# The second pair's query projection behind the first pair's search of maxima, in the tile of the exponentials' sums

## The chip, the cores and the metric

One core of one Trainium2 chip. The metric is the device time of one execution in microseconds, as the median of several runs; a profiled execution gives the trace. Engines: PE is TensorE (PEld its weight loads), DVE is VectorE, ACT is ScalarE, POOL is GpSimd, SP is SyncE, whose queue issues most DMAs.

## The reference

Two layers of a diffusion trunk over 512 latent tokens and 256 context tokens, D_MODEL 1024. Each layer mixes tokens in three branches (pooling, attention, a bidirectional gated recurrence), merges them through gates, and ends with a SwiGLU block. The change lies in the attention of the latent queries (layer 0 also runs the context's). Cut to that:

```python
N_HEADS, N_KV_HEADS, HEAD_DIM = 8, 2, 64
q = rmsnorm(q.reshape(B, L, N_HEADS, HEAD_DIM), q_norm_l)
k = rmsnorm(k.reshape(B, L, N_KV_HEADS, HEAD_DIM), k_norm_l)
if row is not None:
    q = rope_2d(q, row, col)
    k = rope_2d(k, row, col)
...
def _attend(q, k, v):
    s = jnp.einsum('bqhgd,bshd->bhgqs', q, k).astype(jnp.float32) * (HEAD_DIM ** -0.5)
    p = jax.nn.softmax(s, axis=-1).astype(v.dtype)
    return jnp.einsum('bhgqs,bshd->bqhgd', p, v)
```

Latent queries see all 768 keys; context queries (layer 0 only) see the 256 context keys. Everything is float32 at the interface.

## The kernel before, in words

Activations lie feature by feature: a tile holds 128 features by 768 tokens (256 context, then 512 latent). A product with float32 accuracy is made of three matmuls: each operand is split into a rounded part `hi` and a rest `lo` (`load_w`, `split`, `mm3`), so each block of 128x128 weights is loaded by DMA, cast on ScalarE (line 237) and subtracted on VectorE (line 239). Layer 0 works on all 768 tokens, in two segments of 256 and 512 columns, layer 1 on the 512 latent ones.

TensorE's instructions run in the order of the program. On the other engines a planner sets the order: it goes by priority (program order, weight loads lifted far ahead) and by its own simulated times. To keep TensorE busy while the attention waits for other engines, the program keeps a queue of generators of independent work, the **fillers**: the merge of the recurrence's branch and the gates of the attention's branch. `fill(us)` adds credit and emits filler stages until the credit is used up; how much credit stands at each place is written by hand in `PACE`. Filler that isn't used here is run later, so its total does not depend on these credits.

The eight heads are done in four pairs, one tile of 128 features (two heads) each. For every pair:

- `qproj(i)` makes the queries: `qgemm` (product with a 128x1024 weight tile, copied from PSUM by ScalarE, line 932), then `headnorm` (square, `fill(4.5)`, sum over the head by a matmul with `self.blk` at line 347, reciprocal root at lines 294 to 297, scaling at 349) and `rope_lat` (lines 354 to 357 on VectorE).
- `attn_max` searches the row maxima of the scores. Its first step splits the queries (ScalarE line 620, VectorE line 622, ScalarE line 624); then come matmuls at lines 633 and 641 and reductions on VectorE at lines 635 and 643, in steps; the end are four small VectorE operations (lines 647 to 650).
- `attn_rows` transposes the maxima on TensorE (line 659) and puts them into spare rows of an operand (line 662), so that the scores come out with the maximum taken off.
- `attn_pv` computes scores (lines 686, 687), exponentials (line 688, into tiles `e`, three buffers), their sums over the keys (line 690, into a tile `tot`, one buffer) and the product with the values (line 696). The next pair's search and the projection of the pair after it are worked in as hooks.

The first pair has nothing before it to hide in: `attention` splits the keys (`attn_kv`, lines 607 and 609), gives 6.0 us of credit to fillers, starts the first pair's search, projects the second pair, and then lets the search run, with filler between its steps. The second pair's queries lie in a buffer of the tag `e`; the third and fourth pair's in the tag `q`. Tiles of one tag share slots: whoever gets a slot waits for the last user of the tile before it.

Of the kernel before, what the change touches and what calls it, by code (L numbers as in the profile page):

```python
# [11 lines left out]
F32 = mybir.dt.float32  # L12
# [6 lines left out]
P = 128  # L19
# [3 lines left out]
LX = 512  # L23
T = LC + LX
# [18 lines left out]
class Trunk:  # L43
# [680 lines left out]
    def attention(self, l, k, q, qproj, full, ap, bo):  # L724

        c0 = 0 if full else LC
        F, FH, FL = PACE['att'][l], PACE['head'][l], PACE['last'][l]
        self.attn_kv(0, k, ap)
        self.fill(6.0)
        nxt = self.attn_max(0, q, full, ap)  # L730
        next(nxt)
        q = qproj(1)
        for _ in nxt:
            self.fill(PACE['seek'][l])
        self.fill(PACE['rows'][l])
        s = self.attn_rows(0, full)
        self.fill(3.0)
        late = iter(())
        for p in range(4):
            nxt = self.attn_max(p + 1, q, full, ap) if p < 3 else None  # L740
            hi, lo = bo[0][p], bo[1][p]
            oun = Lazy(lambda: self.t(ap, [P, T], F32, "ntmp", bufs=2))
            state = {}

            def hooks(i, half):
                if i > 0 and half == 0:
                    next(late, None)
                if (i, half) == (5, 0):
                    self.now(late)
                    if p < 2:  # L750
                        state["q"] = qproj(p + 2)
                if nxt is not None:
                    if (i, half) == (0, 0) or (1, 1) <= (i, half) < (4, 1):
                        next(nxt, None)
                    elif (i, half) == (4, 1):
                        for _ in nxt:
                            pass
                    elif (i, half) == (5, 1):
                        state["s"] = self.attn_rows(p + 1, full)
                if (i, half) == (3, 1) and p == 0:  # L760
                    self.attn_kv(1, k, ap)
                self.fill(0.5 * (F if nxt is not None else FL))
            sm = Lazy(lambda: self.t(ap, [P, T], F32, "sm"))
            tot = self.attn_pv(p, s, full, ap, oun, sm, hooks)
            late = self.attn_out(c0, oun.get(), tot, sm.get(), hi, lo)
            if p == 3:
                self.now(late)
            self.fill(FH)
            s, q = state.get("s"), state.get("q")
# [73 lines left out]
    def layer(self, l, full, pre):  # L843
# [72 lines left out]
        at = atp.__enter__()  # L916
# [8 lines left out]
        def early(i):  # L925
            return self.t(at, [P, 2, 512], F32, "e", bufs=3).rearrange("p a b -> p (a b)")[:, 0:T]
# [1 line left out]
        def later(i):  # L928
            return self.t(at, [P, T], F32, "ntmp", bufs=2)
        def qgemm(i, bank=None):  # L930
            q = self.t(at, [P, T], F32, "q") if i != 1 else early(0)
            self.now(self.gemm_h(self.load_w(W[22 + i], [P, KD, P]), segs, lambda s0, s1, a: nc.scalar.copy(q[:, s0:s1], a), bank))  # L932
            return q

        def qnorm(i, q):
            scratch = early if i == 0 else later
            self.headnorm(q, q, c0, self.v(l, O_QN, 1), scratch)
            self.rope_lat(q, scratch)
            return q
        q0 = qgemm(0, self.score_bank)  # L940
        self.headnorm(k, k, 0, self.v(l, O_KN, 1), early)
        self.rope_lat(k, later)
        q0 = qnorm(0, q0)

        def qproj(i):
            return qnorm(i, qgemm(i))
# [375 lines left out]
```

## Time and profile before

| | us |
|---|---|
| median of 3 runs | 2128.71 |
| lowest, highest | 2127.93, 4074.69 |
| the profiled execution's own time | 2131.06 |
| its span, first to last instruction | 2129.0 |
| TensorE busy in the span | 2064.9 |
| VectorE busy | 1133.6 |
| ScalarE busy | 681.7 |
| mean granted TensorE clock, share of full | 0.993 |

The profiled execution is 2.35 us above the median, and 2.06 us of it lie outside the span. Busy time of an engine is the time in which it executes; waits and issuing do not count. The highest of the three runs stands by itself and does not move the median.

### The profile page before, as it was taken

What the parts mean: (1) busy time and instruction counts of PE and PEld (TensorE: products, weight loads), DVE (VectorE), ACT (ScalarE), POOL (GpSimd) and SP (SyncE); (2) the same over time, 40 slices, a digit from 0 to 9 for tenths busy, and PEclk for the clock granted to TensorE, in tenths of its full rate; (3) what the DMA queues carried; (4) which work ended last, traced back from release to release, by engine and by line L of the source; (5) the groups of instructions that cost most, each with busy time, mean ns of one, the idle gap of its engine ahead of it and who ended that gap; (6) DMA issues with size and microseconds to landing.
All of it is one profiled execution on the core that took longest, in us unless ns stands there. A gap on an engine that the chain in (4) does not pass through costs nothing.

```text
span 2129.0 us, 28512 instructions
## 1 busy us (share of the span) xinstructions
PE 2064.9 (97%) x11844; PEld 1690.9 (79%) x11844; DVE 1133.6 (53%) x1699; ACT 681.7 (32%) x958; POOL 37.3 (2%) x79
## 2 busy tenths in 40 slices
PE   6998999999999999999999999999899999999999
PEld 4986778777687988888888889778666689888887
DVE  6274635766654676334433354774777665333333
ACT  5323124444332432112112234243444343222221
POOL 0010001000000000000000000001000000000000
PEclk9999999999999999999999999999999999999999
DMA  7203632222154245224423222123322352222332
GB/s 296 80 31 118 211 134 82 100 70 87 52 169 151 90 149 166 91 94 158 140 67 107 85 88 76 60 72 102 104 89 70 113 174 89 96 93 96 103 96 92
DMA packets 75744, 230.92 MB, mean 108 GB/s; under 512 B 8464, under 2 KB 8608, under 8 KB 75488
## 3 DMA queue, kind: packets, MB, share of 16 engines
q1 hardware_dynamic: 75168, 227.57, 32.0%
q8 instruction: 93, 1.52, 0.3%
q0 software_dynamic: 448, 1.54, 0.2%
q14 instruction: 35, 0.29, 0.0%
HBM read 209.16 MB, written 19.92 MB: 108 GB/s over the span
## 4 chain that ended last, share of the span: by engine, by line
PE 88%; DVE 7%; DMA 2%; ACT 2%; issue 1%; SPq 0%; POOL 0%; DVEq 0%; ACTq 0%
PE g L266 64%; PE g L1084 5%; PE att L1084 2%; PE att L377 2%; PE pv L696 2%; PE g L1040 2%; DMA ada<-in_w_ada_dram 1%; PE att L434 1%; PE att L169 1%; DVE AT L473 1%; PE att L686 1%; PE att L687 1%; DVE lo L239 1%; PE att L641 1%; ACT hi L237 1%
## 5 line engine op out<-in xcount | busy, mean ns | idle before, releaser
L266 PE MATMUL g<-h,hi 128*128 128x256 f32 (+1 forms) x3792 | 1002.7, 360 | 8.1 <-ACT e L932 2.8
L266 PEld LDWEIGHTS g<-h,hi 128*128 128x128 f32 x3792 | 673.4, 189 | 150.4 <-issue 33.0
L266 PE MATMUL g<-h,lo 128*128 128x256 f32 (+1 forms) x1896 | 591.2, 355 | 0.0
L237 ACT CAST hi<-raw 128x1024 fp32r<-128x1024 f32 (+1 forms) x237 | 245.4, 1037 | 848.0 <-PE g L266 526.7
L239 DVE TENSOR_TENSOR lo<-raw,hi 128x1024 fp32r<-128x1024 f32 (+1 forms) x237 | 285.6, 1206 | 320.4 <-ACT hi L237 313.3
L266 PEld LDWEIGHTS g<-h,lo 128*128 128x128 f32 x1896 | 358.9, 189 | 50.3 <-issue 2.2
L1098 DVE SCALAR_TENSOR_TENSOR x<-g,mod,x 128x256 f32<-128x256 f32 (+1 forms) x64 | 42.4, 682 | 164.1 <-PE g L266 144.3
L266 PE MATMUL g<-uh,hi 128*128 128x512 f32 (+1 forms) x416 | 129.5, 358 | 0.0
L266 PE MATMUL g<-ul,hi 128*128 128x512 f32 (+1 forms) x416 | 129.5, 358 | 0.0
L266 PE MATMUL g<-uh,lo 128*128 128x512 f32 (+1 forms) x416 | 129.4, 358 | 0.0
L1000 DVE TENSOR_TENSOR sa<-sa,g 128x512 f32<-128x512 f32 (+1 forms) x43 | 35.1, 818 | 169.2 <-PE g L266 168.0
L210 DVE SCALAR_TENSOR_TENSOR junk<-adar,cb 128x1024 f32<-128x1024 f32 x64 | 78.3, 1223 | 36.0 <-DMA adar<-in_w_adaT_dram 35.1
L266 PEld LDWEIGHTS g<-uh,hi 128*128 128x128 f32 x416 | 78.2, 188 | 11.6
L266 PEld LDWEIGHTS g<-uh,lo 128*128 128x128 f32 x416 | 78.2, 188 | 11.6
L266 PEld LDWEIGHTS g<-ul,hi 128*128 128x128 f32 x416 | 78.2, 188 | 11.5
L688 ACT ACTIVATE e<-att 128x512 f32<-128x512 f32 x104 | 56.3, 595 | 90.8 <-PE att L687 90.5
L473 DVE COPY_PREDICATED AT<-masks,att 128x512 f32<-128x512 uint8 (+1 forms) x84 | 48.9, 631 | 14.3 <-PE att L434 14.2
L696 PE MATMUL pv<-e,Vv 128*64 128x512 f32 (+1 forms) x224 | 56.1, 585 | 0.0
L266 PE MATMUL g<-boa,hi 128*128 128x512 f32 (+1 forms) x192 | 52.1, 357 | 1.4 <-DVE tanh L836 1.4
L434 PE MATMUL att<-qq,K 64*128 64x128 f32 x560 | 43.3, 295 | 9.3 <-DVE qq L462 7.0
L434 PEld LDWEIGHTS att<-qq,K 64*128 64x128 f32 x560 | 36.9, 189 | 18.0 <-issue 13.7
L377 PE MATMUL att<-vhi,h 128*128 128x384 f32 x192 | 49.5, 336 | 0.0
(351 smaller groups left out, 2587.4 us busy)
## 6 DMA issues: line engine op xcount, KB each, us to landing
raw<-in_w_fi_dram SPq DMA_DIRECT2D x88, 512.0 KB, 3.5
raw<-in_w_in_dram SPq DMA_DIRECT2D x84, 512.0 KB, 3.5
adar<-in_w_adaT_dram SPq DMA_DIRECT2D x48, 512.0 KB, 4.2
ada<-in_w_ada_dram SPq DMA_DIRECT2D x64, 256.0 KB, 4.0
raw<-in_w_fo_dram SPq DMA_DIRECT2D x34, 448.0 KB, 3.3
raw<-in_w_out_dram SPq DMA_DIRECT2D x18, 512.0 KB, 4.2
ada<-in_w_ada_dram SPq DMA_DIRECT2D x16, 512.0 KB, 10.2
raw<-in_w_fo_dram SPq DMA_DIRECT2D x16, 512.0 KB, 3.5
```

Of the source, the lines that this page charges most:

```text
L210: i = nc.vector.scalar_tensor_tensor(out=junk, in0=raw, scalar=1.0, in1=cb[:, v, :], op0=ALU.mult, op1=ALU.mult, accum_out=rows[:, f, v:v ...
L237: nc.scalar.copy(hi, raw)
L239: nc.vector.tensor_sub(lo, raw, hi.bitcast(F32))
L266: nc.tensor.matmul(ps.part(s0, s1), w, x[:, s0:s1], start=(first and i == 0), stop=(last and i == 2))
L377: nc.tensor.matmul(ps[:, :384], self.h[x][kk][:, c], w[:, kk, :], start=(kk == 0 and i == 0), stop=(kk == KD - 1 and i == 2))
L434: nc.tensor.matmul(pt[hd][:, i, :], K(ph, g0 + i), Q(ph, g0 + i), start=True, stop=True)
L473: scores(plain(K), lambda ph, c: pick(qq, c * P, P, h, ph), grow, lambda o, i, n: nc.vector.copy_predicated(o, mk.to_broadcast([P, n, P]), i))
L688: nc.scalar.activation(e[:, o, :], pst, AF.Exp, scale=0.125)
L696: nc.tensor.matmul(out[64 * o:64 * o + 64, :n], w(sk), es[i][:, o, u * n:(u + 1) * n], start=(start and u == 0), stop=(stop and u == len(j ...
L1040: nc.tensor.matmul(o, w[:, kk, :], self.h[x][kk][:, tg[0]:tg[1]], start=(kk == 0 and i == 0), stop=(kk == KD - 1 and i == 2))
L1084: self.nc.tensor.matmul(ps, w[:, i, :], xs[y][:, g0:g1], start=(i == 0 and k == 0), stop=(i == nk - 1 and k == 2))
L1098: self.nc.vector.scalar_tensor_tensor(out=x[:, s0:s1], in0=ps, scalar=g[:, d, v:v + 1], in1=x[:, s0:s1], op0=ALU.mult, op1=ALU.add)
```

## The change

`qproj(1)` is moved from before the steps of the first pair's search to behind them, and its result is put into the first 768 elements of a tile of the tag `tot`, in place of one of the tag `e`. The search's first step, the split of the first pair's queries, stays where it is. In `attention`, `qproj(1)` was followed by the search's steps; now it stands between them and the credit `PACE['rows']`.

```diff
         nxt = self.attn_max(0, q, full, ap)
         next(nxt)
-        q = qproj(1)
         for _ in nxt:
             self.fill(PACE['seek'][l])
+        q = qproj(1)
         self.fill(PACE['rows'][l])
         s = self.attn_rows(0, full)
...
         def qgemm(i, bank=None):
-            q = self.t(at, [P, T], F32, "q") if i != 1 else early(0)
+            q = self.t(at, [P, T], F32, "q") if i != 1 else self.t(at, [P, 2, LX], F32, "tot").rearrange("p a b -> p (a b)")[:, 0:T]
```

The credits are unchanged: `PACE['seek']` is 2.0 us a step in layer 0 and 1.2 in layer 1 (seven steps and six), `PACE['rows']` is 3.0 and 3.5.

## Rows read from the trace of the kernel before

**Rows 1.** The profile's page: busy time of the engines, and the chain that ended last.

```profile
PE 2064.9 (97%) x11844; PEld 1690.9 (79%) x11844; DVE 1133.6 (53%) x1699; ACT 681.7 (32%) x958; POOL 37.3 (2%) x79
...
PE 88%; DVE 7%; DMA 2%; ACT 2%; issue 1%; SPq 0%; POOL 0%; DVEq 0%; ACTq 0%
```

**Rows 2.** Timeline of TensorE, layer 1 (start, us, engine, line, what, count [idle before <-releaser]).

```profile
1499.17 0.61 PE L266 MATMUL g<-h,hi 128*128 128x512 f32 x2
...
1510.58 0.50 PE L266 MATMUL g<-h,hi 128*128 128x512 f32 x1 [2.83 <-ACT e L932]
...
1513.65 1.76 PE L347 MATMUL att<-ntmp,cm 128*128 128x512 f32 x2
...
1515.35 0.50 PE L633 MATMUL att<-khh,qs 64*128 64x256 f32 x4
...
1534.52 0.27 PE L659 MATMUL att<-cm,m 128*64 128x128 f32 x1 [3.38 <-DVE m L650]
...
1545.36 0.51 PE L633 MATMUL att<-khh,qs 64*128 64x256 f32 x4
```

**Rows 3.** Timeline of TensorE, layer 0.

```profile
362.67 0.28 PE L266 MATMUL g<-h,lo 128*128 128x256 f32 x1
...
373.78 0.39 PE L266 MATMUL g<-h,hi 128*128 128x256 f32 x1 [0.62 <-DVE tanh L836]
...
376.39 1.52 PE L347 MATMUL att<-ntmp,cm 128*128 128x256 f32 x4
...
377.83 0.50 PE L633 MATMUL att<-khh,qs 64*128 64x256 f32 x4
...
401.97 0.27 PE L659 MATMUL att<-cm,m 128*64 128x128 f32 x1 [1.14 <-DVE m L650]
...
404.95 0.40 PE L686 MATMUL att<-qs,khh 128*128 128x512 f32 x1
...
411.97 0.50 PE L633 MATMUL att<-khh,qs 64*128 64x256 f32 x4
```

**Rows 4.** Timeline of ScalarE, layer 0.

```profile
370.46 1.69 ACT L620 CAST qs<-q 64x768 fp32r<-64x768 f32 x2 [4.42 <-DVE q L357]
```

**Rows 5.** Timeline of VectorE, layer 0.

```profile
369.74 0.69 DVE L357 TENSOR_TENSOR q<-q,e 128x512 f32<-128x512 f32 x1
...
410.38 1.22 DVE L690 TENSOR_TENSOR tot<-e,e 128x1024 f32<-128x1024 f32 x1 [5.67 <-ACT e L688]
```

**Rows 6.** Timeline of ScalarE, layer 1.

```profile
1506.45 0.62 ACT L620 CAST qs<-q 64x512 fp32r<-64x512 f32 x1 [0.36 <-DVE q L357]
1506.98 1.04 ACT L237 CAST hi<-raw 128x1024 fp32r<-128x1024 f32 x1
1508.05 0.62 ACT L620 CAST qs<-q 64x512 fp32r<-64x512 f32 x1
```

**Rows 7.** Stages of layer 1: us, busy PE, PEld, DVE, ACT, POOL, PEclk, DMA share, GB/s.

```profile
1512.00:1513.00 1.00, 1.00 (x4) 0.81 (x3) 0.00 (x0) 0.99 (x1) 0.00 (x0) 0.50 0.61 227
1515.00:1516.00 1.00, 1.00 (x6) 0.52 (x6) 0.05 (x1) 0.55 (x1) 0.00 (x0) 0.93 0.44 92
```

**Rows 8.** Timeline of TensorE, third pair's projection, layer 0.

```profile
446.35 1.45 PE L347 MATMUL att<-ntmp,cm 128*128 128x256 f32 x4
...
450.16 0.30 PE L659 MATMUL att<-cm,m 128*64 128x128 f32 x1
```

**Rows 9.** Timeline of VectorE, third pair, layer 0.

```profile
452.20 0.95 DVE L662 TENSOR_TENSOR qs<-att,misc 12x768 fp32r<-12x768 f32 x1
```

**Rows 10.** Timeline of ScalarE, third pair, layer 0.

```profile
457.06 1.69 ACT L620 CAST qs<-q 64x768 fp32r<-64x768 f32 x2 [1.21 <-DVE q L357]
```

**Rows 11.** Timeline of TensorE, third pair, layer 1.

```profile
1573.86 1.02 PE L347 MATMUL att<-ntmp,cm 128*128 128x512 f32 x2
...
1590.07 0.50 PE L633 MATMUL att<-khh,qs 64*128 64x256 f32 x3 [0.26 <-ACT qs L620]
```

**Rows 12.** The profile's page: DMA issues (KB each, median us to landing).

```profile
raw<-in_w_in_dram SPq DMA_DIRECT2D x84, 512.0 KB, 3.5
```

## The prediction

> **What bounds the kernel now.** I read the engines' busy line first. TensorE is busy for 2064.9 of 2129.0 us and the chain that ended last is 88% TensorE [rows 1], so at most 64 us of the span are free of matmuls, and the fillers that run in the cracks of the attention are work that must be done anyway. Their sum does not change when a block is moved. So an idle microsecond of TensorE in the attention is a microsecond of time, unless another idle one goes away. The Trainium skill ("Perfetto Trace Analysis", Identifying the Most-Contended Engine) says that busy matmul time is a bad measure of nearness to the limit, and that weight loading is a better one. By its measure TensorE is at 79% [rows 1] and a stall might be made good elsewhere. Against that speaks the spacing of the 512-column matmuls: two take 0.61 us where one takes 0.40 [rows 2, 3], so 0.21 us each, which is 512 columns at 2.4 GHz. Nothing in that stretch can be run faster later.
>
> Second I read the timelines of TensorE, VectorE and ScalarE around line 633, the first matmul of the search of maxima, in both layers. TensorE's order is the program's order; the other engines' order is the planner's. Before the search TensorE runs filler (credit 6.0), the second pair's projection, filler (credit 4.5) and its norm's sum. Meanwhile VectorE finishes the keys' and the first pair's rotary chain, and ScalarE waits for it before it can split the queries that the search reads: 4.42 us of waiting in layer 0 [rows 4]. So the projection is what covers this chain.
>
> **The change, part by part.** It adds and removes no instruction; it moves one block (24 or 48 matmuls, copies from PSUM, a square, the sum by matmul, the reciprocal root, the rotary operations, and one 512 KB weight load with its split) behind the search, and gives its result the slot of `tot`.
>
> *The cover that goes, layer 0.* The projection starts at about 362.6; between it and the search lie projection, filler and norm sum, to 377.83, some 15 us [rows 3]. Now the search's first matmul is next at 362.6, and needs the split of line 620, whose two parts run from 370.46 to 372.15, started by the rotary add of 369.74 [rows 4, 5]. No step of that chain depends on the moved block. TensorE therefore stands until 372.15: **+9.5 us**. Its first matmul may start with the first part, at 371.3 (low end 8.7).
>
> *The same, layer 1.* The ten filler stages of credit 6.0 (30 matmuls) end at 1499.4, inside the first row of [rows 2], where the projection starts. The split's parts start at 1506.45 and 1508.05, with a weight cast of 1.04 us between them [rows 6]. That cast follows slots that the projection and the filler behind it free; while TensorE stands, it isn't ready, so I put the second part at 1507.0 to 1507.6: **+8.2 us** (9.3 if the cast stays).
>
> *Waits that go.* Layer 0: 1.14 us at line 659, which waited for the maxima's last step, since that stood behind the second pair's operations and the fillers' on VectorE, and 0.62 us at a filler [rows 3]; with the projection in between, the maxima are long done. Layer 1: 3.38 us at line 659 likewise, and 2.83 us at a filler that wanted the PSUM bank of the projection, whose copy was queued behind the split on ScalarE [rows 2]. After the search ScalarE has no such queue. **-1.8 and -6.2 us.**
>
> *The clock.* Behind the 2.83 us wait the granted clock is at 0.50, the 1.2 GHz level, from 1512, and it is back at 0.93 in 1515 to 1516 [rows 7]: some 3.4 us at half speed, 1.7 us lost. After 9 us of standing it is low at the restart at least as long, and I take 1.7 us for each stall, 3.4 at most. The Trainium skill ("TensorE: Matmul & The Clock Gate", What's actually happening) says that the slow level is the array's resting state and that activity lifts it; the rows agree, though no run here shows a rest as long as these. Layer 0 has no such stretch now: **+1.7**. Layer 1 has two, behind 2.83 and behind 3.38 us, and keeps one: **-1.7**.
>
> *The cover of the moved block.* Its projection now runs with the search behind it, so its chain has to be done when the second pair's search begins. Layer 0: between the norm's sum and that search lie the sum (1.4), filler 3.0, and 411.97 - 401.97 = 10.0 us [rows 3], 14.4 in all. The nearest rows are those of the third pair, whose projection stands in the same company: 446.35 to 457.06 + 1.69, 12.4 us [rows 8, 10]. Covered, by 2.0. Layer 1: sum 0.9 (1.7 at half clock), filler 3.5 and 10.8 [rows 2], of which 1.7 is slow clock, so 13.5; the third pair took 1573.86 to 1590.07, 16.2 us [rows 11], among more VectorE work (sums, reciprocals) than there is here. I take **+1.0**, between 0 and 4. The maxima's rows (line 662) now run inside the second pair's chain. For the third pair that took from 450.16 to 452.20 + 0.95, 3.0 us [rows 8, 9]; here the first score comes 2.98 us behind line 659 [rows 3]. Zero, at most 1.
>
> *The shared tile.* The first sum of exponentials writes `tot`, and must wait until the moved queries have been read, by line 624 last. It is due 8.4 us behind line 659 [rows 3, 5], so 12.8 behind the start of the norm's sum; the reads end, by the third pair's rows, at 12.4 + 1.7 = 14.1. It comes some 1.5 us late, and behind it on VectorE stand the reductions of the second pair's search, due at 14.9, and the fourth score's exponential buffer. Zero for TensorE, up to 3 a layer. The buffer of `e` that is freed was never waited for: zero.
>
> *The queues.* On SP one weight load passes behind two or three filler weights. It lands 3.5 us after issue [rows 12] and its cast takes 1.04 [rows 6]; loads are issued far ahead, into slots, and TensorE waits for none here. Zero; 4.5 us if it came too late. POOL's fill of the maxima does not move.
>
> **The sum.** Layer 0: 9.5 - 1.8 + 1.7 = +9.4. Layer 1: 8.2 - 6.2 - 1.7 + 1.0 = +1.3. Together +10.7 on the profiled execution's 2131.06, 2.35 above the median of 2128.71: 2141.8 there, **2139** as a median. The ends: 8.7 - 1.8 and 8.2 - 6.2 - 3.4, so +5; and 9.5 - 1.8 + 3.4 + 4 with 9.3 - 6.2 + 4, so +22.
>
> **The rivals.** *Covered after all, or paid back (not slower, 2122 to 2132).* The planner orders VectorE anew. If it took the four subtractions of line 609 and a weight's split out of the first pair's rotary chain, the chain would end up to 5 us sooner; the waits that go (8.0) and the slow stretch (1.7) would then be worth more than two stalls of 4. For it: VectorE is full there and those subtractions are only needed by the scores. Against: up to the stall VectorE sees the same instructions with the same readiness. The slack that the skill's measure would leave goes here too: by it the 10.7 us shrink towards 0.
>
> *The wait moves on (slower than forecast, 2145 to 2155).* The moved chain is late for the second pair's search, and the late first sum holds VectorE, so that PSUM tiles and exponential buffers come late: 3 to 4 us in each layer, and a second slow stretch of 1.7. It decides if chain and reads take more than 14 us from the norm's sum on. For it: the third pair's 16.2 us in layer 1. Against: the same third pair waits only 0.26 us at the last [rows 11].
>
> *Over 2% slower* (2171 or more) would take 43 us; no wait or queue in these rows has a price like that.
>
> **How the numbers follow.** Forecast (2134 to 2145) 0.58, the wait moves on 0.25, covered or paid back 0.13, anything beyond 2% 0.04. The range reaches up through the second case and down over the upper part of the third: 2130 to 2153. A difference of 2% (43 us) is what this comparison can tell from no change, and my forecast is 0.5%: faster by over 2% 0.01, within 0.96, slower 0.03.
>
> **What would show it.** In the profile after: a wait of TensorE at line 633 for line 620 of 8 to 10 us, in each layer and once, with a granted clock of 0.50 behind it; no wait at line 659 for the first pair; a short wait at the second pair's line 633 at most in layer 1; the first `tot` write released by line 624. I am wrong if line 620 comes well before 370 or 1506, if the wait is there and TensorE's total idle time has not grown, or if SP's weight for the moved block comes late.

## The result, and the profile after

The changed kernel takes 2141.05 us, the median of four runs (2140.06 to 2143.2), against 2128.32 for the kernel before, the median of four. The ratio is 1.0065, 95% interval 1.0052 to 1.0077: 11 to 16 us slower, which is within 2% but clear of no change. One of the four runs of the kernel before, at 4074.69 us, stands by itself and is left out of the ratio. The profiled execution took 2141.0 us.

The page of the profile after, its span and its busy line:

```profile
span 2138.9 us, 28513 instructions
...
PE 2064.1 (97%) x11844; PEld 1689.4 (79%) x11844; DVE 1134.7 (53%) x1699; ACT 681.2 (32%) x958; POOL 37.2 (2%) x79
```

TensorE is busy for 2064.1 us, as much as before [rows 1], but the span is 9.9 us longer. So its idle time grew, by 10.7 us. The timeline of TensorE in layer 0 shows where:

```profile
369.45 0.58 PE L633 MATMUL att<-khh,qs 64*128 64x256 f32 x1 [8.60 <-ACT qs L620]
...
370.30 0.79 PE L633 MATMUL att<-khh,qs 64*128 64x256 f32 x3 [0.28 <-ACT qs L620]
...
403.97 1.46 PE L347 MATMUL att<-ntmp,cm 128*128 128x256 f32 x4
...
408.74 0.27 PE L659 MATMUL att<-cm,m 128*64 128x128 f32 x1
...
409.86 0.38 PE L266 MATMUL g<-h,hi 128*128 128x256 f32 x1 [0.85 <-ACT tanh L792]
...
412.83 0.40 PE L686 MATMUL att<-qs,khh 128*128 128x512 f32 x1
...
420.20 0.50 PE L633 MATMUL att<-khh,qs 64*128 64x256 f32 x4
```

The search's first matmul (line 633), which started without a wait in [rows 3], waits 8.60 us and, after its first piece, 0.28 more. The waits of 1.14 us at line 659 and of 0.62 at a filler in [rows 3] are gone, and one of 0.85 at another filler is new. ScalarE and VectorE at the same place (the last row of each belongs to what comes below):

```profile
368.57 1.68 ACT L620 CAST qs<-q 64x768 fp32r<-64x768 f32 x2 [5.44 <-DVE q L357]
...
419.76 1.68 ACT L624 CAST qs<-tot 64x768 fp32r<-64x768 f32 x2
```

```profile
367.84 0.69 DVE L357 TENSOR_TENSOR q<-q,e 128x512 f32<-128x512 f32 x1
...
412.76 0.95 DVE L662 TENSOR_TENSOR qs<-att,misc 12x768 fp32r<-12x768 f32 x1
...
422.13 1.22 DVE L690 TENSOR_TENSOR tot<-e,e 128x1024 f32<-128x1024 f32 x1
```

The rotary add at line 357 is followed by the split at line 620, and by the search, as in [rows 4, 5]. The whole chain stands 1.9 us earlier than before, and so does everything else from the first pair's norm sum on (352.50 against 354.38), since the stages ahead of the attention took a little less in this execution. Layer 1, TensorE and ScalarE:

```profile
1515.22 1.43 PE L633 MATMUL att<-khh,qs 64*128 64x256 f32 x4 [7.54 <-ACT qs L620]
...
1537.31 0.50 PE L266 MATMUL g<-h,hi 128*128 128x512 f32 x1 [0.49 <-ACT tot L932]
...
1540.17 1.02 PE L347 MATMUL att<-ntmp,cm 128*128 128x512 f32 x2
...
1544.46 0.27 PE L659 MATMUL att<-cm,m 128*64 128x128 f32 x1
...
1554.43 0.38 PE L633 MATMUL att<-khh,qs 64*128 64x256 f32 x1 [0.66 <-ACT qs L620]
...
1555.07 0.50 PE L633 MATMUL att<-khh,qs 64*128 64x256 f32 x3 [0.26 <-ACT qs L620]
```

```profile
1514.55 1.26 ACT L620 CAST qs<-q 64x512 fp32r<-64x512 f32 x2 [6.10 <-DVE q L357]
```

Line 633 waits 7.54 us for the split. Line 659 has no wait in place of 3.38, and the filler that waited 2.83 us for the projection's bank waits 0.49 [rows 2]. The second pair's search waits 0.66 and 0.26 us. The granted clock (the third column from the right) in slices of 1 us behind both waits:

```profile
372.00:373.00 1.00, 1.00 (x6) 0.90 (x5) 0.85 (x2) 0.00 (x0) 0.00 (x0) 0.50 0.00 0
...
373.00:374.00 1.00, 1.00 (x5) 0.82 (x4) 0.13 (x1) 0.00 (x0) 0.00 (x0) 0.72 0.00 0
...
1519.00:1520.00 1.00, 1.00 (x3) 0.81 (x4) 1.00 (x2) 0.00 (x0) 0.00 (x0) 0.50 0.00 0
...
1520.00:1521.00 1.00, 1.00 (x5) 0.67 (x3) 0.27 (x1) 0.39 (x1) 0.00 (x0) 0.78 0.00 0
```

At 0.50 TensorE runs at 1.2 GHz. The level lasts to 373.56 in layer 0 (0.28 of a loss of 0.50 in the slice to 374) and to 1520.44 in layer 1, so 4.1 and 5.2 us from the restart on, half of which is lost.

### The profile page after: what moved, and what is told of

Read it like the earlier page. It is cut to its first block, busy times and chain, and to the rows that moved or that the text cites. A ratio compares the mean times of both kernels' runs of the same rounds, so it can differ in the third digit from the quotient of the medians.

```text
span 2138.9 us, 28513 instructions
## 1 busy us (share of the span) xinstructions
PE 2064.1 (97%) x11844; PEld 1689.4 (79%) x11844; DVE 1134.7 (53%) x1699; ACT 681.2 (32%) x958; POOL 37.2 (2%) x79
## 5 line engine op out<-in xcount | busy, mean ns | idle before, releaser
L473 DVE COPY_PREDICATED AT<-masks,att 128x512 f32<-128x512 uint8 (+1 forms) x84 | 48.8, 630 | 12.7 <-PE att L434 12.5
```

Source lines behind the costliest of these rows:

```text
L473: scores(plain(K), lambda ph, c: pick(qq, c * P, P, h, ph), grow, lambda o, i, n: nc.vector.copy_predicated(o, mk.to_broadcast([P, n, P]), i))
```

## The experiments

The kernel before ran beside each of them; its medians there were 2128.41, 2127.94 and 2129.11 us. Intervals are 95%.

**1. The order alone.** The moved block keeps its new place, its queries go into a buffer of `e` again.

```diff
-            q = self.t(at, [P, T], F32, "q") if i != 1 else self.t(at, [P, 2, LX], F32, "tot").rearrange("p a b -> p (a b)")[:, 0:T]
+            q = self.t(at, [P, T], F32, "q") if i != 1 else early(0)
```

> The projection stands behind the search, as in the changed kernel, but its queries lie in a buffer of the tag e, as before. Theory (the search waits bare for the first pair's rotary chain): the same waits of about 8.6 and 7.5 us at line 633, and 2139 to 2143 us, equal to the changed kernel within 2 us. Rival (the shared tile makes the first sum of exponentials late and costs): 3 to 6 us less than the changed kernel, 2135 to 2138. A third possibility, that the shared tile helps, would show as 2144 or more.

Measured: 2141.93 us, ratio 1.0071 (1.0055 to 1.0088); waits at line 633 of 8.9 us in layer 0 and 9.1 in layer 1, of which 7.54 are at the first pair's search. The order alone does all that the change does. Lines 659 on TensorE and 690 on VectorE (the first write of `tot`), layer 0 and then layer 1, belong to what comes below:

```profile
408.15 0.27 PE L659 MATMUL att<-cm,m 128*64 128x128 f32 x1
...
1544.03 0.27 PE L659 MATMUL att<-cm,m 128*64 128x128 f32 x1
```

```profile
421.55 1.22 DVE L690 TENSOR_TENSOR tot<-e,e 128x1024 f32<-128x1024 f32 x1
...
1553.20 1.22 DVE L690 TENSOR_TENSOR tot<-e,e 128x1024 f32<-128x1024 f32 x1
```

**2. The tile alone.** The order of before, with the queries in `tot`.

```diff
-            q = self.t(at, [P, T], F32, "q") if i != 1 else early(0)
+            q = self.t(at, [P, T], F32, "q") if i != 1 else self.t(at, [P, 2, LX], F32, "tot").rearrange("p a b -> p (a b)")[:, 0:T]
```

> The order of before, with the second pair's queries in the tile of the sums. Theory: no wait of TensorE changes, 2126 to 2131 us, the first write of tot a little later at most. Rival (shared tile): 3 to 6 us above before, 2131 to 2135, with TensorE waiting behind VectorE at the first pair's scores.

Measured: 2127.95 us, ratio 0.9998 (0.9988 to 1.0007). TensorE's waits in layer 1 are those of [rows 2]:

```profile
PE att L659 <- DVE m L650: 3.4, 1, 3.4
...
PE g L266 <- ACT tot L932: 2.8, 1, 2.8
```

The shared tile costs nothing. In layer 0 it doesn't even delay the first write of `tot`, which comes 13.4 us behind line 659 with the tile (422.13 and 408.74, kernel after) and without it (421.55 and 408.15, experiment 1): VectorE has the second pair's chain ahead of it in both. In layer 1 that write comes 12.7 us behind line 659 in the kernel after and 9.2 in experiment 1, so there the tile makes it 3.5 us later. TensorE pays nothing for that: its waits from 1485 to 1600 us come to 9.5 us with the tile and 9.8 without. The write in the kernel after:

```profile
1557.17 1.23 DVE L690 TENSOR_TENSOR tot<-e,e 128x1024 f32<-128x1024 f32 x1
```

**3 and 4. More filler ahead of the search**, 16.0 us of credit in place of 6.0, and 11.0 in the other kernel.

```diff
-        self.fill(6.0)
+        self.fill(16.0)
```

> The changed kernel with 16.0 us of filler credit ahead of the search in place of 6.0. Theory, if filler costs nothing: the waits at line 633 vanish (16.4 us) with the slow clock behind them (3.8 and 5.4 us at half speed, 4.6 us), 2119 to 2124 us, below before. Rival (filler is a finite stock, and what is used here is missing at the end of the attention): the same waits vanish, but up to 10 us a layer come back as waits of TensorE in the last pair, 2128 to 2140. If neither the waits nor the time go, the theory has fallen.

> The changed kernel with 11.0 us of filler credit ahead of the search. Theory (a finite stock of filler, that runs out at the end of the attention): waits at line 633 of about 4 and 2.5 us; at the end of the attention waits for line 287 between none and 2 us in layer 0 and about 2 in layer 1; 2128 to 2135 us. If filler were free: 2129 to 2131 with no new wait at the end.

Measured: 2129.98 us with 16.0 (1.0009; 1.0000 to 1.0018) and 2137.87 with 11.0 (1.0045; 1.0031 to 1.0058). TensorE's waits with 16.0 us in layer 0, first around the search, then at the end of the attention:

```profile
PE att L687 <- DVE qs L662: 1.6, 1, 1.6
...
PE att L633 <- ACT e L688: 0.8, 1, 0.8
```

```profile
PE g L266 <- ACT boa L287: 5.2, 1, 5.2
```

and at the end of layer 1's attention, with 16.0 first and with 11.0 second:

```profile
PE g L1084 <- ACT y L287: 5.1, 1, 5.1
...
PE g L266 <- ACT boa L287: 3.3, 1, 3.3
```

```profile
PE g L1084 <- ACT y L287: 4.9, 1, 4.9
...
PE g L266 <- ACT boa L287: 3.6, 1, 3.6
```

The waits for line 620 at the first pair's search are gone with 16.0, but at the end TensorE waits for line 287, the split of the last pair's output, for which neither the kernel before nor the kernel after waits (the rows with `y` are the same line in the merge that follows; there the kernel after waits 3.5 us for a DMA). The stock of filler is fixed, and what is used early is missing there. In the window from 600 to 640 us, where TensorE was busy throughout before, it is busy for 34.6 of 40 us with 16.0, at a mean clock of 0.91. With 11.0 the search still waits 2.3 us in layer 0 and 2.5 in layer 1. Layer 1 pays at the end as with 16.0; layer 0 pays nothing there, but waits 1.2 us for the bank of the moved product.

The time with 11.0 is worse than I had put it (2128 to 2135). Its page has TensorE busy for 2069.9 us of a span of 2135.2, against 2062.8 of 2127.5 with 16.0 and 2064.1 of 2138.9 in the kernel after. So TensorE stands idle 9.5 us less than in the kernel after, about as little as with 16.0, but the same number of matmuls takes 5.8 us more. The granted clock is at 0.50 (1.2 GHz) behind even short waits of this execution: from 1511 to 1517 us behind the 2.25 us at the search of layer 1, and from 651 to 654 behind one of 1.87 us in the merge of layer 0. I had counted the waits and not this.

**5. Credit moved, not added.** The changed kernel with the credits of the second pair's norm (4.5) and of the rows (3.0 or 3.5) given ahead of the search.

```diff
-        self.fill(6.0)
+        self.fill(10.5 + PACE['rows'][l])
...
         q = qproj(1)
-        self.fill(PACE['rows'][l])
...
-            self.headnorm(q, q, c0, self.v(l, O_QN, 1), scratch)
+            self.headnorm(q, q, c0, self.v(l, O_QN, 1), scratch, 'none' if i == 1 else 'hna')
```

> The changed kernel with filler credit moved, not added: the 4.5 us of the second pair's norm and the 3.0 or 3.5 of the rows are given ahead of the search (13.5 and 14.0 in place of 6.0), and none is left at their old places. Theory (bare chain, and a finite stock of filler): waits at line 633 of 1 to 2 us in layer 0 and none in layer 1, no new waits at line 287 at the end of the attention, new waits of some 2 us a layer for the square ahead of the norm's sum, and at the second pair's search; 2126 to 2134 us. Rival (what came back at the end with added credit was not the missing filler): waits at line 287 of 3 to 5 us at the end as with the added credit, 2130 to 2138.

Measured: 2128.27 us, ratio 1.0002 (0.9992 to 1.0011). Layer 1's attention:

```profile
PE att L347 <- ACT ntmp L341: 2.3, 1, 2.3
...
PE att L633 <- ACT qs L620: 2.0, 4, 1.1
```

The first pair's search waits in neither layer (the 2.0 us are the second and third pair's), and there is no wait for line 287 at the end. The loss is repaid by filler alone, without the projection; what the second pair's norm lacks costs 2.3 us in layer 1 and 2.5 in layer 0 (line 347 waits for the square) where 4.5 us of credit had stood.

**6. The product ahead, the norm behind.** The moved block is cut behind its product (part 1 is the product, part 2 the norm and the rotary operations).

```diff
         next(nxt)
+        q = qproj(1, 1)
         for _ in nxt:
             self.fill(PACE['seek'][l])
-        q = qproj(1)
+        q = qproj(1, 2, q)
```

> The moved block is cut in two: the product of the second pair's projection stays ahead of the search, its norm and rotary operations stand behind it. Theory (matmuls ahead of the search are the cover, 8.1 us in layer 0 and 5.5 in layer 1): the wait at line 633 shrinks to 1 to 2 us in layer 0 and 2.5 to 4 in layer 1; the wait at line 659 stays away; 2122 to 2128 us. Rival (the norm with its filler and the late chain of the second pair is what costs, not the missing product): 2137 to 2142, like the changed kernel.

Measured: 2126.07 us, ratio 0.9988 (0.9979 to 0.9998). The first matmul of the search in both layers:

```profile
371.95 0.38 PE L633 MATMUL att<-khh,qs 64*128 64x256 f32 x1 [0.29 <-ACT qs L620]
...
1508.05 0.38 PE L633 MATMUL att<-khh,qs 64*128 64x256 f32 x1 [2.12 <-ACT qs L620]
```

Of the first waits 0.29 and 2.12 us are left, of 8.60 and 7.54 (behind the first piece come 0.47 and 0.26 more). They shrank by 8.3 and 5.4 us, and the product's matmuls are 8.1 and 5.5: these matmuls were the cover.

**7 and 8. A longer chain**, in the kernel after and in the kernel before: four more operations on VectorE behind the first pair's rotary add. They take the maximum of the queries with themselves.

```diff
         q0 = qnorm(0, q0)
+        for _ in range(4):
+            nc.vector.scalar_tensor_tensor(out=q0[:, c0:], in0=q0[:, c0:], scalar=1.0, in1=q0[:, c0:], op0=ALU.mult, op1=ALU.max)
```

> The changed kernel with four more operations on VectorE at the end of the first pair's rotary chain (the maximum of the queries with themselves, which changes no value): some 4 times 0.95 us in layer 0 and 4 times 0.7 in layer 1. Theory (TensorE stands until this chain ends): the waits at line 633 grow by the same, to about 12.3 and 10.3 us, and the time to 2146 to 2151 us. Rival (TensorE waits for something else at the same place, or the wait has slack): the time stays at 2139 to 2143.

> The kernel before with the same four operations. Theory (the second pair's projection covers this chain, with 5.7 us to spare in layer 0 and 6.7 in layer 1): within 2 us of before, 2126 to 2131. Rival (VectorE sets the pace there whatever TensorE does): 2132 to 2136, as much more than before as the changed kernel's copy of this shows.

Measured, after: 2149.75 us (1.0097; 1.0083 to 1.0111), 8.7 above the kernel after, which was timed at another time (6.8 by the two ratios to the kernel before, 1.0097 and 1.0065). The search's first matmul in both layers:

```profile
371.71 0.58 PE L633 MATMUL att<-khh,qs 64*128 64x256 f32 x1 [12.57 <-ACT qs L620]
...
1521.12 1.43 PE L633 MATMUL att<-khh,qs 64*128 64x256 f32 x4 [10.45 <-ACT qs L620]
```

12.57 and 10.45 against 8.60 and 7.54: TensorE waits 4.0 and 2.9 us longer, and the operations take 3.93 us in layer 0 and 2.87 in layer 1. Every microsecond on this chain is a microsecond of TensorE. Measured, before: 2124.74 us (0.9984; 0.9975 to 0.9994), so the same operations cost nothing there. They even gain 3.2 us, and the time lies below what I expected (2126 to 2131). TensorE and ScalarE in layer 1:

```profile
1512.89 0.38 PE L633 MATMUL att<-khh,qs 64*128 64x256 f32 x1 [1.28 <-ACT qs L620]
...
1523.02 0.50 PE L641 MATMUL att<-khh,qs 64*128 64x512 f32 x1 [1.11 <-DVE mx L643]
...
1531.54 0.27 PE L659 MATMUL att<-cm,m 128*64 128x128 f32 x1
```

```profile
1506.29 0.58 ACT L932 COPY e<-g 128x512 f32<-128x512 f32 x1
...
1512.23 1.25 ACT L620 CAST qs<-q 64x512 fp32r<-64x512 f32 x2
```

The projection's copy (line 932) now stands ahead of the split on ScalarE, at 1506.29 where it stood behind it; the wait of 2.83 us for its bank and the 3.38 us at line 659 [rows 2] are gone, and waits of 1.28 and 1.11 us stand for them. All waits of TensorE from 1485 to 1600 us come to 4.3 us there, against 7.2 in the kernel before.

**9. Only the norm's sum behind the search.** TensorE's order of before, except that the second pair's sum over the head and all behind it follow the search; the square (in part 1) and its 4.5 us of filler stay ahead.

```diff
         next(nxt)
+        q = qproj(1, 1)
+        self.fill(PACE['hna'])
         for _ in nxt:
             self.fill(PACE['seek'][l])
-        q = qproj(1)
+        q = qproj(1, 2, q)
...
```

> The order of before on TensorE up to the second pair's norm: product, square and 4.5 us of filler stay ahead of the search, and only the sum over the head, the reciprocal root and the rotary operations stand behind it. No filler credit is added. Theory (matmuls ahead of the search cover the first pair's chain; the second pair's norm in the middle of the search was what made line 659 wait in before): no wait at line 633 for the first pair and none over 1 us at line 659, 2116 to 2124 us, 5 to 12 us below before. Rival (the late norm of the second pair makes its own search late, by more than the waits that go): 2128 to 2136.

Measured: 2124.17 us, ratio 0.9979 (0.9970 to 0.9988), just above the 2116 to 2124 that I expected. Layer 1's attention (line numbers are one to three higher here: 634 for 633, 935 for 932):

```profile
PE g L266 <- ACT tot L935: 2.8, 1, 2.8
...
PE att L634 <- ACT qs L621: 1.6, 4, 0.7
```

No wait for the first pair's maxima is left; the wait for the fillers' bank is. The 1.6 us are at the searches of the second and third pair. The granted clock stays at 1.00 from 1495 to 1530 us, also behind the 2.8 us wait, where it fell to 0.50 in [rows 7].

**10. The same with the product in a bank of the scores** (the edit against experiment 9).

```diff
-                q, sq = qgemm(i), later(0)
+                q, sq = qgemm(i, self.score_bank), later(0)
```

> The kernel with only the second pair's norm sum and what follows behind the search, and its product in a PSUM bank of the scores instead of one of the fillers'. Theory (the 2.8 us wait in layer 1 is for the fillers' bank, which the late copy holds): that wait goes, 2120 to 2123 us. Rival (the search then wants the bank of the scores): the wait moves to line 633, 2123 to 2127.

Measured: 2120.23 us, ratio 0.9968 (0.9955 to 0.9980). Layer 1's attention:

```profile
PE att L634 <- ACT qs L621: 1.6, 4, 0.7
```

The 2.8 us are gone and nothing stands for them. By time alone the step from experiment 9 isn't clear of noise (the two intervals overlap); the wait that is gone shows it. This version beats both kernels: 2120.23 against 2129.11 beside it, and 2141.05.

## Why the prediction was right

It said 2139 us, 2130 to 2153, with a bare wait at the search's head as the cause. Its terms against the profile after, in us:

| term | predicted | measured |
|---|---|---|
| wait at line 633, layer 0 | +9.5 | +8.9 (8.60 + 0.28) |
| waits that go, layer 0 | -1.8 | -0.9 (1.14 and 0.62 go, 0.85 comes at 409.86) |
| slow clock, layer 0 | +1.7 | +2.0 (half of 4.1) |
| wait at line 633, layer 1 | +8.2 | +7.5 |
| waits that go, layer 1 | -6.2 | -5.7 (2.83 becomes 0.49) |
| slow clock, layer 1 | -1.7 | -0.8 (half of 5.2, less 3.4) |
| second pair's search, layer 1 | +1.0 | +0.9 (0.66 + 0.26) |
| sum | +10.7 | +11.9 |

From the first pair's norm sum to the last pair's sum of exponentials (line 776) layer 0 takes 10.1 us longer and layer 1 2.4: from 354.38 to 600.04 and from 1491.65 to 1679.13 before, from 352.50 to 608.27 and from 1499.78 to 1689.63 after. That is 12.5 us, and the medians differ by 12.7. The two profiled executions differ by only 9.9, since that of the kernel before was 2.35 above its median and slower outside these stretches. The ends of the stretch in layer 0, before and after, and the slow clock behind the 3.38 us wait of layer 1 before:

```profile
354.38 1.45 PE L347 MATMUL att<-e,cm 128*128 128x256 f32 x4
...
600.04 1.08 PE L776 MATMUL att<-tot,cm 128*64 128x512 f32 x4
```

```profile
352.50 1.45 PE L347 MATMUL att<-e,cm 128*128 128x256 f32 x4
...
608.27 1.08 PE L776 MATMUL att<-tot,cm 128*64 128x512 f32 x4
```

```profile
1536.00:1537.00 1.00, 1.00 (x4) 0.80 (x3) 0.97 (x3) 0.58 (x1) 0.00 (x0) 0.50 0.48 176
```

The sum is nearer than its terms: the two waits at line 633 came out 1.3 us shorter than forecast and the other terms 2.5 us dearer, and these cancel in part.

*The cover that goes* was right in kind and near in size: in layer 0 the first matmul started with the first part of the split, as in the low end (8.7), and in layer 1 the wait of 7.54 us lies below the 8 to 10 named as a sign. Experiments 7 and 8 show the chain to be what TensorE waits for, and experiments 5 and 6 show that any matmuls ahead of the search, the product's or the fillers', cover it. In layer 1 the weight cast that stood between the two parts of the split is gone, as argued: they run back to back from 1514.55.

*The waits that go* went, but for 0.49 and a new one of 0.85 us for a tanh on ScalarE. *The clock* was under-sized by 0.3 and 0.9 us: TensorE's restart stays slow for 4.1 and 5.2 us where I took 3.4. That layer 1 had two slow stretches to lose was a matter of the one execution read: in experiment 2, with the waits of before, the clock falls behind the 3.35 us wait (0.50 from 1529 to 1532) and stays at 1.00 behind the one of 2.81, as it does in experiment 9 behind 2.83.

*The cover of the moved block*: in layer 0 the chain took longer than the third pair's rows said (from 403.97 to the end of the split at 419.74, 15.8 us against 12.4), but so did TensorE's way to the second pair's search at 420.20, which had no wait. The rows of line 662 ended at 413.71, 5.0 us behind line 659 and not 3.0, and a score matmul waited some 0.2 us for them (413.76, where 413.53 was due). *The shared tile*: the first sum came at 422.13, 13.4 us behind line 659 where it stood 8.4 behind it in [rows 3, 5]. It is 5 us late, not 1.5, and not for the reason given, since it is as late without the shared tile (experiment 1); only in layer 1 does the tile delay it, by 3.5 us. Nor does the trace show it released by line 624, a sign that I had named: in both layers it follows a reduction of the second pair's search (line 635) without a gap. It costs nothing, as experiments 1 and 2 show. *The queues*: around neither search does TensorE wait for a DMA.

*The rivals.* The wait did not move on to the second pair beyond what the forecast held, and no planner's order covered the first pair's chain. The Trainium skill ("Perfetto Trace Analysis", Identifying the Most-Contended Engine) names the share of weight loading, not busy matmul time, as a measure of nearness to the limit. My rival drawn from it, that the slack in this share makes a stall good, would have given a time near 2129. Here idle time was paid in full, as the longer chain shows (7), with weight loading at 79% before and after. But filler brought forward is missing elsewhere: that the credit is a stock with an end to it (3, 4, 5) the prediction had only in the sentence that the fillers' sum does not change.

## What to carry to other kernels

Work that stands in front of a dependent matmul in an in-order queue is cover, even where it looks like a delay: before moving it, measure the other engines' chain that it hides, and move only the part that delays the search's later steps (here the norm, and not the product). Filler put in its place comes out of a fixed stock, so credit is moved, and what it covered at the end is looked at again. A late copy out of PSUM can hold up work that has nothing to do with it, through the bank (2.8 us here, experiments 9 and 10).

## What the runs showed that I had not expected

Four operations added to the critical chain of the kernel before made it 3.2 us faster (ratio 0.9984, 0.9975 to 0.9994), and in its trace ScalarE copies the projection's result out of its bank before the split, not after. That the planner chose that order because the split was ready later, and that the gain comes from it, is argued from the timeline; it was not tried by itself, though experiment 10, which takes the bank out of the way, removes the same wait.

With 11.0 us of credit the waits for the split shrank from 17.7 us (8.9 in layer 0, 8.8 in layer 1 with the later pairs') to 4.8, and the time by 3.2 only: the rest went into waits at the end of the attention and into matmuls at the slow clock, also behind waits of 1.87 and 2.25 us. So a short wait can cost more than its length, and whether it does differs from execution to execution.
